# Other byte offsets for the matmul operands of a hybrid transformer block on one core

## The chip, the cores and the metric

The kernel runs on one core of a Trainium2 chip. The metric is the device time of one execution in microseconds, taken as the median of several runs. Each number of a trace comes from one profiled execution, whose span is the time from its first to its last instruction.

An SBUF address, in this document, is the byte at which a tile begins within its partition. All 128 partitions have the same layout, so one number says where a tile lies.

## The reference

One block of a hybrid network on 512 tokens with 1024 features, in fp32: a normalization, one wide input projection, two token mixers side by side (a gated delta rule with 8 heads and a retention with 4 heads), a gated sum of both, an output projection with a residual, and an MLP of width 4096 with a residual.

```python
xn = rmsnorm(x, n_mix_pre)
proj = xn @ w_in                       # 512 x 1024 by 1024 x 14352
qa, ka, va, za, beta_logit, a_dt, qb, kb, vb, gb, gate_a, gate_b = _split_cols(proj, IN_SIZES)
...
oa = chunk_gated_delta_rule(qa, ka, va, beta, g)
oa = rmsnorm(oa, norm_a) * jax.nn.silu(za)
ya = oa @ w_br_a
...
ob = chunk_retention(qb, kb, vb)
ob = rmsnorm(ob, norm_b) * jax.nn.silu(gb)
yb = ob @ w_br_b
mix = (jax.nn.sigmoid(gate_a) * ya + jax.nn.sigmoid(gate_b) * yb) @ w_out
x = x + rmsnorm(mix, n_mix_post)
hn = rmsnorm(x, n_mlp_pre)
ff = jnp.square(jax.nn.relu(hn @ w_up)) @ w_down
return x + rmsnorm(ff, n_mlp_post)
```

Most of the work is in the products with `w_in`, `w_br_a`, `w_br_b`, `w_out`, `w_up` and `w_down`.

## The kernel before

Every large product is made of three matmuls. A factor is split in two halves of type fp32r, a rounded one (`hi`) and the rest (`lo`), and `mm3` (lines 78 to 83) adds hi x hi (L81), hi x lo (L82) and lo x hi (L83) into one PSUM tile. The first operand of `nc.tensor.matmul` behind the output is the stationary one, which a LDWEIGHTS loads into the array ahead of the matmul (128 columns, 512 bytes of a partition); the second is the moving one, which streams through (mostly 512 columns, 2048 bytes of a partition). The trace names a matmul as output<-moving,stationary: `mm<-actT,whi` streams `actT` past weights from `whi`.

`weights` (lines 85 to 105) brings one block of weights: a DMA of 512 KB from SP's queue into a `raw` tile, ScalarE's rounding copy into `whi` (L100), VectorE's subtraction into `wlo` (L101). `whi` and `wlo` have three buffers each in the pool `ring`, so this work runs ahead of the matmuls by up to three blocks; a new block waits until the matmuls of the block three before it have ended. In a few places the halves go to other tiles, which the trace names `keep`.

Three functions use these blocks:

- `feature_major` (lines 107 to 125): the weights are stationary, the features move. The features are `actT` (two tiles of 8 x 512 columns, hi and lo; the normalized input in the first part of the kernel, later `mix` or the hidden layer), `og` (two tiles of 4 x 512 columns, a head's gated output) or `hn` (the normalized input of the MLP).
- `token_major` (lines 127 to 143): the features are stationary, the weights move. The trace shows `mm<-whi,actT` or `mm<-whi,ff`, where `ff` is the hidden layer. For two of the four groups of the MLP the hidden layer lies in a pair of `actT` tiles, for the other two in a pair of `og` tiles (first half) and a pair of tiles of the pool `pm` (second half).
- `row_tiles` (lines 824 to 850): as `token_major`, but with weights that stay on chip in `keep` tiles, for the output projection and the last group of the MLP.

Smaller products have no part in the change's own tiles: the transposes (L179), the plain fp32 products of the delta rule (L442 to L626), and the two products of retention, `dl<-qr,kr` and `dl<-vr,s`, which are `mm3` on tiles of the pool `pb`.

The order of instructions on each engine is made by a scheduler when the program is built, by the program's order and the priority that `weights` asks for. Tiles are laid out in SBUF pool after pool in the order in which pools are opened: constants (`cp`), `ring`, `act` (`actT` and `og`), `sm`, then a pool for each of the four parts, one after the other in the same space. A tile's address is therefore settled by the sizes of all the tiles before it, each rounded up to 32 bytes.

Of the kernel before, what the change touches and what calls it, by code (L numbers as in the profile page):

```python
# [10 lines left out]
F32 = mybir.dt.float32  # L11
F32R = mybir.dt.float32r
# [7 lines left out]
P = 128  # L20
# [7 lines left out]
OFF_GA, OFF_GBR = 12304, 13328  # L28
DFF = 4096


# [29 lines left out]
def hybrid_block_kernel(ctx: ExitStack, tc: tile.TileContext, a: dict, out: bass.AP):  # L61
# [5 lines left out]

    cp = ctx.enter_context(tc.tile_pool(name="cp", bufs=1))
    ring = ctx.enter_context(tc.tile_pool(name="ring", bufs=3))
    raw_pools = [ring]  # L70
# [5 lines left out]
    dr = ctx.enter_context(tc.tile_pool(name="dr", bufs=2, space=DRAM))  # L76

    def mm3(ps, lhs, rhs, first, last):
        lh, ll = lhs
        rh, rl = rhs  # L80
        nc.tensor.matmul(ps, lh, rh, start=first, stop=False)  # L81
        nc.tensor.matmul(ps, lh, rl, start=False, stop=False)  # L82
        nc.tensor.matmul(ps, ll, rh, start=False, stop=last)  # L83

    def weights(src, k0, nk, c0, ncols, keep=None):
        """nk blocks of 128 rows, ncols columns, in exact halves; split ahead of other work that is due."""
        n = nk * ncols
        i = next(loads)
        raw = raw_pools[i % len(raw_pools)].tile([P, 1024], F32, tag="raw", name="raw", bufs=2)
        nc.sync.dma_start(  # L90
            raw[:, :n].rearrange("p (k c) -> p k c", k=nk),
            src[k0 * P : (k0 + nk) * P, c0 : c0 + ncols].rearrange("(k p) c -> p k c", p=P),
        )
        if keep is None:
            hi = ring.tile([P, 1024], F32R, tag="whi", name="whi")
            lo = ring.tile([P, 1024], F32R, tag="wlo", name="wlo")
        else:
            hi, lo = keep
        with tc.high_priority(200 if i >= 6 else 0):
            nc.scalar.copy(hi[:, :n], raw[:, :n])  # L100
            nc.vector.tensor_tensor(lo[:, :n], raw[:, :n], hi[:, :n], ALU.subtract)  # L101
        return (
            hi[:, :n].rearrange("p (k c) -> p k c", k=nk),
            lo[:, :n].rearrange("p (k c) -> p k c", k=nk),
        )

    def feature_major(src, xs, c0, ncols, kts, krow0=0):
        """[feature, token] products of ncols columns: PSUM tiles of 128 features."""
        nf = ncols // P
        pss = [psm.tile([P, xs[0].shape[2]], F32, tag="mm", name="mm") for _ in range(nf)]  # L110
        step = 1024 // ncols
        for k0 in range(0, kts, step):
            wh, wl = weights(src, krow0 + k0, step, c0, ncols)
            for f in range(nf):
                fs = slice(f * P, (f + 1) * P)
                for kk in range(step):
                    kt = k0 + kk
                    mm3(
                        pss[f],
                        (wh[:, kk, fs], wl[:, kk, fs]),  # L120
                        (xs[0][:, kt, :], xs[1][:, kt, :]),
                        kt == 0,
                        kt == kts - 1,
                    )
        return pss

    def token_major(src, lhs, c0, kts, krow0=0):
        """[token, 512 columns] products: one PSUM tile for each 128 tokens."""
        pss = [psm.tile([P, T], F32, tag="mm", name="mm") for _ in range(4)]
        for k0 in range(0, kts, 2):  # L130
            wh, wl = weights(src, krow0 + k0, 2, c0, 512)
            for t in range(4):
                tt = slice(t * P, (t + 1) * P)
                for kk in range(2):
                    kt = k0 + kk
                    mm3(
                        pss[t],
                        [x[:, tt] for x in lhs(kt)],
                        (wh[:, kk, :], wl[:, kk, :]),
                        kt == 0,  # L140
                        kt == kts - 1,
                    )
        return pss
# [4 lines left out]
    def rsqrt(xv, n, name):  # L148
        """1/sqrt of a positive [P, n] tile."""
        yi = sm.tile([P, n], I32, tag=f"rs_i{n}", name="rs_i")  # L150
        y = sm.tile([P, n], F32, tag=f"rs_{name}", name="rs_y")
        t = sm.tile([P, n], F32, tag=f"rs_t{n}", name="rs_t")
        nc.vector.tensor_scalar(yi, xv.bitcast(I32), 1, None, ALU.logical_shift_right)
        nc.vector.tensor_scalar(y.bitcast(I32), yi, -1, 1597463007, ALU.mult, ALU.add)
        for _ in range(3):
            nc.vector.scalar_tensor_tensor(t, y, -0.5, y, ALU.mult, ALU.mult)
            nc.vector.tensor_tensor(t, t, xv, ALU.mult)
            nc.vector.scalar_tensor_tensor(y, t, 1.5, y, ALU.add, ALU.mult)
        return y
# [4 lines left out]

# [1 line left out]
    cmat = cp.tile([P, 3 * P], F32, name="cmat")  # L166
# [13 lines left out]

# [1 line left out]
    xs = [act.tile([P, 8, T], F32R, tag="actT", name="actT") for _ in range(2)]  # L182
    acc = cp.tile([P, 8, T], F32, name="acc")
# [7 lines left out]
    def root(v):  # L191
        """1/sqrt of a positive [P, n] tile."""
        n = v.shape[1]
# [9 lines left out]
    def rows_to_features(xn, t, dst):  # L203
        """Transposes the [128 tokens, 1024] tile into the halves dst."""
        tt = slice(t * P, (t + 1) * P)
# [9 lines left out]
    with tc.tile_pool(name="xp", bufs=2) as xp:  # L215
# [62 lines left out]

# [1 line left out]
        baT = xp.tile([16, T], F32, tag="baT", name="baT")  # L280
# [44 lines left out]
    def gate_rows(pss, o_t, zt):  # L325
        """o * rstd * silu(z) in place, token-major."""
        for t in range(4):
# [25 lines left out]

# [1 line left out]
    def conv_silu(ps, ch, dst, pool):  # L355
# [28 lines left out]
    def decays(h, pool):  # L384
        """exp(sum of g over (m, c]) for m <= c, else 1: [m, chunk, c]."""
        pd = psx.tile([P, T], F32, tag="dl", name="dl", bufs=3)
# [18 lines left out]
    with tc.tile_pool(name="pa", bufs=1) as pa:  # L405
# [46 lines left out]
        def base_inverse(g4, pool):  # L452
            """Unit lower triangular inverses of 64 diagonal 32-blocks, one to a partition."""
            scr_m, scr_r, scr_t = (dr.tile([4, 16, 1024], F32, tag=f"scr{i}", name="scr") for i in range(3))
# [33 lines left out]
        def double_blocks(pool, scr_r, m0):  # L488
            """From 32-blocks to the transposed 128-block inverses, for two heads."""
            rn = pool.tile([P, 8, 64], F32, tag="qf", name="rn", bufs=2)  # L490
# [42 lines left out]
        def values_queries(g2, pool):  # L533
# [33 lines left out]
            )  # L567
            # r_q * dk**-0.5
            rq = pool.tile([P, 8], F32, tag="rq", name="rq", bufs=2)
# [4 lines left out]
        def recurrence(g2, vq, pool):  # L574
# [61 lines left out]

            # rstd of the true output r_q * dk**-0.5 * o; a half of it for silu(z)
            v = pool.tile([P, 8], F32, tag="ov", name="ov")
# [40 lines left out]

# [1 line left out]
    with tc.tile_pool(name="pb", bufs=1) as pb_:  # L681
# [107 lines left out]
        for half in range(2):  # L789
# [5 lines left out]
            for f in range(4):  # L795
# [3 lines left out]
                nc.vector.tensor_tensor(acc[:, ft, :], acc[:, ft, :], m, ALU.add)  # L799
        mix = [act.tile([P, 8, T], F32R, tag="actT", name="actT") for _ in range(2)]  # L800
        for half, pss in branch_partial(w_br[1], prev, 12):
# [9 lines left out]

# [1 line left out]
    with tc.tile_pool(name="pm", bufs=1) as pm:  # L813
# [10 lines left out]
        def row_tiles(src, lhs, krow0, keeps, done):  # L824
            """[token, 1024] products, two tiles of 128 tokens and then one by one; the weights stay on chip."""
            kept = {}
# [27 lines left out]
        def norm_halves(parts):  # L854
            """rstd of rows that come in two halves; what else is done with a half may follow it."""
            ss = sm.tile([P, 2], F32, tag="nh_s", name="nh_s")
# [9 lines left out]
        def add_normed(t, parts, w):  # L866
            """x2[t] += rmsnorm(parts) * w."""
            fw = pm.tile([P, D], F32, tag="ym", name="fw", bufs=2)
# [58 lines left out]
        for grp in range(4):  # L927
            if grp % 2:
                whole = [act.tile([P, 8, T], F32R, tag="actT", name="actT") for _ in range(2)]
                ff = [[w[:, 4 * half : 4 * half + 4, :] for w in whole] for half in range(2)]  # L930
            else:
                ff = [
                    [act.tile([P, 4, T], F32R, tag="og", name="ff") for _ in range(2)],
                    [pm.tile([P, 4, T], F32R, tag=f"ff{i}", name="ff") for i in range(2)],
                ]
# [62 lines left out]
```

## Time and profile before

| What | Value |
|---|---|
| median of 3 runs | 1413.96 us (1412.99 to 1417.39) |
| span of the profiled execution | 1410.7 us |
| TensorE (PE) busy | 1394.6 us, 99% of the span |
| weight loads (PEld), beside the matmuls | 1139.7 us, 81% |
| VectorE (DVE) busy | 809.0 us, 57% |
| ScalarE (ACT) busy | 571.7 us, 41% |
| GpSimd (POOL) busy | 53.0 us, 4% |
| DMA | 129.74 MB, 92 GB/s on the mean |

The page gives no time of the profiled execution beyond its span. In its rows a group is named by line, engine, operation and tiles (written<-read), with the number of instructions, the time in which at least one of them ran, and the mean duration of one. Matmuls overlap: the next one starts before the one before it has ended, so the mean duration is longer than the distance between two starts. The order of time gives the start of each instruction in microseconds from the start of the span, to 10 ns; a distance between starts is worked out from the first and the last of many.

### The profile page before, as it was taken

Reading aid. Unit: us, or ns where it says so; the run is one execution under the profiler, and the core shown is the slowest. Engines: PE = TensorE matmul, PEld = TensorE weight load, DVE = VectorE, ACT = ScalarE, POOL = GpSimd, SP = SyncE. Lnnn points to the kernel's source line nnn. Section 1 sums busy time; section 2 is a strip of 40 time slices with the busy share of each in tenths; the row PEclk is TensorE's granted clock in tenths of the full one; section 3 lists DMA queues with packets and bytes.
Section 4 is the critical chain, followed back from the end, with each engine's and each line's share of the span. In section 5 each row is a group of like instructions: output and inputs, shape, how many; then the busy total and the mean of one; then the engine's idle time right before and its main releaser. Section 6 shows DMA issues by size and latency. Waiting matters only on the chain.

```text
span 1410.7 us, 17493 instructions
## 1 busy us (share of the span) xinstructions
PE 1394.6 (99%) x6766; PEld 1139.7 (81%) x6766; DVE 809.0 (57%) x1463; ACT 571.7 (41%) x1082; POOL 53.0 (4%) x100
## 2 busy tenths in 40 slices
PE   8999999999999999999999999999999999999997
PEld 6888787878888888888888888888888888888886
DVE  5599889944765564436445455445685333343445
ACT  6778564624534233233342323223464333132331
POOL 1111300200000000000000000000000000000000
PEclk9999999999999999999999999999999999999999
DMA  5232412221221342333223232232724232232321
GB/s 157 75 95 75 114 31 75 73 76 46 89 90 48 103 135 83 97 95 93 75 90 98 75 90 90 75 90 75 238 90 135 90 101 94 92 102 90 108 72 60
DMA packets 69942, 129.74 MB, mean 92 GB/s; under 512 B 4608, under 2 KB 18066, under 8 KB 69859
## 3 DMA queue, kind: packets, MB, share of 16 engines
q1 hardware_dynamic: 66128, 119.03, 26.8%
q0 software_dynamic: 3008, 8.34, 2.1%
q8 instruction: 53, 0.87, 0.3%
q10 hardware_dynamic: 722, 1.25, 0.2%
q14 instruction: 31, 0.25, 0.1%
HBM read 124.93 MB, written 3.67 MB: 91 GB/s over the span
## 4 chain that ended last, share of the span: by engine, by line
PE 92%; DVE 5%; ACT 1%; issue 1%; DMA 1%; SPq 0%; DVEq 0%; ACTq 0%
PE mm L81 27%; PE mm L82 27%; PE mm L83 27%; PE tr L179 2%; DVE c_y L367 1%; PE dl L83 1%; PE dl L82 1%; PE dl L81 1%; PE dl L598 1%; PE dl L626 1%; DVE wlo L101 1%; PE dl L590 1%; PE dl L606 1%; PE dl L619 1%; DVE tmp L473 1%
## 5 line engine op out<-in xcount | busy, mean ns | idle before, releaser
L101 DVE TENSOR_TENSOR wlo<-raw,whi 128x1024 fp32r<-128x1024 f32 x208 | 254.3, 1223 | 387.8 <-ACT whi L100 386.6
L100 ACT CAST whi<-raw 128x1024 fp32r<-128x1024 f32 x208 | 218.3, 1050 | 514.0 <-PE mm L82 282.1
L82 PE MATMUL mm<-actT,whi 128*128 128x512 f32 (+1 forms) x528 | 207.7, 393 | 1.2 <-DVE actT L213 1.2
L81 PE MATMUL mm<-actT,whi 128*128 128x512 f32 (+1 forms) x528 | 206.8, 393 | 1.0 <-ACT actT L212 1.0
L83 PE MATMUL mm<-actT,wlo 128*128 128x512 f32 (+1 forms) x528 | 207.3, 393 | 0.0
L81 PE MATMUL mm<-whi,actT 128*128 128x512 f32 x472 | 185.9, 394 | 0.1
L82 PE MATMUL mm<-wlo,actT 128*128 128x512 f32 x472 | 185.4, 393 | 0.0
L83 PE MATMUL mm<-whi,actT 128*128 128x512 f32 x472 | 185.2, 393 | 0.0
L81 PEld LDWEIGHTS mm<-actT,whi 128*128 128x128 f32 x528 | 99.8, 189 | 21.4 <-ACT actT L212 1.3
L82 PEld LDWEIGHTS mm<-actT,whi 128*128 128x128 f32 x528 | 100.1, 190 | 20.4 <-DVE actT L213 1.4
L83 PEld LDWEIGHTS mm<-actT,wlo 128*128 128x128 f32 x528 | 100.0, 189 | 19.0
L81 PE MATMUL mm<-hn,whi 128*128 128x512 f32 (+1 forms) x288 | 106.3, 370 | 0.6 <-DVE r L921 0.5
L82 PE MATMUL mm<-hn,whi 128*128 128x512 f32 (+1 forms) x288 | 106.2, 369 | 0.0
L83 PE MATMUL mm<-hn,wlo 128*128 128x512 f32 (+1 forms) x288 | 106.0, 369 | 0.0
L81 PEld LDWEIGHTS mm<-whi,actT 128*128 128x128 f32 x472 | 88.6, 188 | 19.0 <-ACT c_y L365 0.5
L83 PEld LDWEIGHTS mm<-whi,actT 128*128 128x128 f32 x472 | 88.6, 188 | 18.2
L82 PEld LDWEIGHTS mm<-wlo,actT 128*128 128x128 f32 x472 | 88.6, 188 | 17.9
L81 PE MATMUL mm<-og,whi 128*128 128x512 f32 x256 | 100.3, 392 | 0.0
L82 PE MATMUL mm<-og,whi 128*128 128x512 f32 x256 | 99.6, 389 | 0.0
L83 PE MATMUL mm<-og,wlo 128*128 128x512 f32 x256 | 98.5, 390 | 0.0
L367 DVE SCALAR_TENSOR_TENSOR c_y<-c_raw,convw,c_y 128x512 f32<-128x512 f32 x96 | 70.5, 752 | 3.4 <-ACT c_y L365 2.8
L81 PEld LDWEIGHTS mm<-hn,whi 128*128 128x128 f32 x288 | 54.0, 187 | 11.4 <-issue 0.7
(286 smaller groups left out, 2077.0 us busy)
## 6 DMA issues: line engine op xcount, KB each, us to landing
raw<-in_w_in_dram SPq DMA_DIRECT2D x113, 512.0 KB, 3.6
raw<-in_w_up_dram SPq DMA_DIRECT2D x36, 512.0 KB, 3.6
raw<-in_w_down_dram SPq DMA_DIRECT2D x32, 512.0 KB, 3.6
raw<-in_w_br_a_dram SPq DMA_DIRECT2D x16, 512.0 KB, 3.6
raw<-in_w_br_b_dram SPq DMA_DIRECT2D x16, 512.0 KB, 3.6
raw<-in_w_out_dram SPq DMA_DIRECT2D x8, 512.0 KB, 3.7
x<-in_x_dram SPq DMA_DIRECT2D x4, 512.0 KB, 6.4
acc<-in_x_dram POOLq DMA_DIRECT2D x4, 512.0 KB, 3.8
```

What stands on the lines that cost most here:

```text
L81: nc.tensor.matmul(ps, lh, rh, start=first, stop=False)
L82: nc.tensor.matmul(ps, lh, rl, start=False, stop=False)
L83: nc.tensor.matmul(ps, ll, rh, start=False, stop=last)
L100: nc.scalar.copy(hi[:, :n], raw[:, :n])
L101: nc.vector.tensor_tensor(lo[:, :n], raw[:, :n], hi[:, :n], ALU.subtract)
L179: nc.tensor.transpose(ps, src, ident)
L367: nc.vector.scalar_tensor_tensor(y, raw[:, j : j + T], tap(j), y, ALU.mult, ALU.add)
L473: nc.vector.tensor_tensor(t3, mb3[:, j, j + 1 : 32].unsqueeze(2).to_broadcast([64, nr, ni]), rb3[:, j, 0:ni].unsqueeze(1).to_broadcast([64 ...
L590: nc.tensor.matmul(ks[:, hh, :], kf[:, h0 + hh, cs], state[:, hh, :], start=True, stop=True)
L598: nc.tensor.matmul(px[:, hh, :], rt[:, nn[hh], :], vx[:, hh, :], start=True, stop=True)
L606: nc.tensor.matmul(pc[:, hh, :], kd[:, nn[hh], :], vn[:, hh, :], start=True, stop=True)
L619: nc.tensor.matmul(qs[:, hh, :], qf[:, hh, cs], prev[:, hh, :], start=True, stop=True)
```

## The change

It adds 56 fp32 columns (224 bytes) of an unused tile at the start of the pool `cp`, and 8 fp32 columns (32 bytes) behind each `whi`, `wlo` and `actT` tile. The columns that are added are neither written nor read. All the rest of the program, its instructions, shapes, buffers and order, is the same; what differs is the address of nearly every tile.

```diff
+STAGGER = 8
...
     cp = ctx.enter_context(tc.tile_pool(name="cp", bufs=1))
+    cp.tile([P, 56], F32, name="shift")
     ring = ctx.enter_context(tc.tile_pool(name="ring", bufs=3))
...
+    def features_tile(name):
+
+        w = act.tile([P, 8 * T + STAGGER], F32R, tag="actT", name=name)
+        return w[:, : 8 * T].rearrange("p (k t) -> p k t", k=8)
...
-            hi = ring.tile([P, 1024], F32R, tag="whi", name="whi")
-            lo = ring.tile([P, 1024], F32R, tag="wlo", name="wlo")
+            hi = ring.tile([P, 1024 + STAGGER], F32R, tag="whi", name="whi")
+            lo = ring.tile([P, 1024 + STAGGER], F32R, tag="wlo", name="wlo")
...
-    xs = [act.tile([P, 8, T], F32R, tag="actT", name="actT") for _ in range(2)]
+    xs = [features_tile("actT") for _ in range(2)]
...
-        mix = [act.tile([P, 8, T], F32R, tag="actT", name="actT") for _ in range(2)]
+        mix = [features_tile("actT") for _ in range(2)]
...
-                whole = [act.tile([P, 8, T], F32R, tag="actT", name="actT") for _ in range(2)]
+                whole = [features_tile("actT") for _ in range(2)]
```

The addresses in the built programs, in bytes, whole and modulo 512. Every operand of a matmul begins at a multiple of 512 bytes from the start of its tile (a column block of 128 fp32, or a row of 512), so the modulo of the tile is that of each operand in it.

| Tile | before | mod 512 | after | mod 512 |
|---|---|---|---|---|
| `raw`, 2 buffers | 36896, 40992 | 32, 32 | 37120, 41216 | 256, 256 |
| `whi`, 3 buffers | 45088, 49184, 53280 | 32, 32, 32 | 45312, 49440, 53568 | 256, 288, 320 |
| `wlo`, 3 buffers | 57376, 61472, 65568 | 32, 32, 32 | 57696, 61824, 65952 | 352, 384, 416 |
| `actT`, hi and lo | 69664, 86048 | 32, 32 | 70080, 86496 | 448, 480 |
| `og`, hi and lo | 102432, 110624 | 32, 32 | 102912, 111104 | 0, 0 |
| `hn`, hi and lo | 128736, 145120 | 224, 224 | 129216, 145600 | 192, 192 |
| `ff` of pool pm, hi and lo | 161504, 169696 | 224, 224 | 161984, 170176 | 192, 192 |
| `qr`, `kr`, `vr`, `s` (retention) | | 224 | | 192 |
| `later` (stationary of L391) | 18624 | 192 | 18848 | 416 |
| `kf`, `kd`, `rt` (delta rule) | 120544, 136928, 153312 | 224 | 121024, 137408, 153792 | 192 |
| end of the SBUF in use | 228384 | | 228864 | |

`keep` tiles lie in the space of `og`, `ff`, `hn` and `facc` and have their offsets.

## The prediction

> **What bounds the kernel now.** I read the page's busy times first, then the granted clock, then the chain that ended last, then the groups kept apart by shape.
>
> ```profile
> span 1410.7 us, 17493 instructions
> PE 1394.6 (99%) x6766; PEld 1139.7 (81%) x6766; DVE 809.0 (57%) x1463; ACT 571.7 (41%) x1082; POOL 53.0 (4%) x100
> PEclk9999999999999999999999999999999999999999
> PE 92%; DVE 5%; ACT 1%; issue 1%; DMA 1%; SPq 0%; DVEq 0%; ACTq 0%
> PE mm L81 27%; PE mm L82 27%; PE mm L83 27%; PE tr L179 2%; DVE c_y L367 1%; PE dl L83 1%; PE dl L82 1%; PE dl L81 1%; PE dl L598 1%; PE dl L626 1%; DVE wlo L101 1%; PE dl L590 1%; PE dl L606 1%; PE dl L619 1%; DVE tmp L473 1%
> ```
>
> TensorE is busy 99% of the span at full clock, and the three matmuls of `mm3` (L81 to L83) make 81% of the chain. There is almost no idle time to win or lose, so the time is the number of these matmuls times the distance from the start of one to the start of the next. A matmul's mean duration (some 390 ns) says little, because they overlap. The distance has to be taken from start times:
>
> ```profile
> 587.03 0.39 PE L81 MATMUL mm<-actT,whi 128*128 128x512 f32 x1
> 630.33 0.40 PE L83 MATMUL mm<-actT,wlo 128*128 128x512 f32 x1
> ```
>
> These are the first and the last of 192 matmuls in one unbroken stretch: 43.30 us / 191 = 226.7 ns. Here both operands stand at byte 32 of 512 (the table in the section on the change). The stretches with other offsets lie in the MLP:
>
> ```profile
> 1103.84 0.39 PE L81 MATMUL mm<-whi,ff 128*128 128x512 f32 x1
> 1114.83 0.39 PE L81 MATMUL mm<-whi,ff 128*128 128x512 f32 x1
> 1125.70 0.39 PE L81 MATMUL mm<-whi,ff 128*128 128x512 f32 x1
> 1136.69 0.39 PE L81 MATMUL mm<-hn,whi 128*128 128x512 f32 x1
> 1181.49 0.39 PE L81 MATMUL mm<-whi,actT 128*128 128x512 f32 x1
> ```
>
> From 1103.84 to 1114.83 lie 48 matmuls, the moving operand at byte 32 and the stationary one at 224 (`ff` tiles of pool pm): 10.99 / 48 = 229.0 ns. From 1114.83 to 1125.70 lie 48 more of the same line and tile names, but now `ff` is a pair of `og` tiles at byte 32: 10.87 / 48 = 226.5 ns. From 1125.70 it is 224 again: 10.99 / 48 = 229.0 ns. From 1136.69 to 1181.49 lie 192 with moving `hn` at 224 and stationary `whi` at 32: 44.80 / 192 = 233.3 ns. Same shape, same clock, no idle time: what differs is the byte offset. The mean duration of one, in windows of the pure stretches, marks the same difference; the third row is from the view of one tile (least, median, most):
>
> ```profile
> L81 PE MATMUL mm<-actT,whi 128*128 128x512 f32 x64 | 24.9, 389 | 0.0
> L81 PE MATMUL mm<-hn,whi 128*128 128x512 f32 x64 | 25.2, 394 | 0.0
> L81 PE MATMUL dl<-vr,s x40: 389/389/391, 536.4 to 886.3; 128*128 128x512 f32 x40
> ```
>
> `vr` and `s` both stand at 224 and last as long as two operands at 32. So it is not the place of one operand that goes with the time but the difference. I call moving minus stationary, modulo 512, the phase: 0 costs 226.7 ns, 192 costs 233.3, 320 costs 229.0.
>
> Why the operands can meet at all:
>
> ```profile
> 590.21 0.39 PE L83 MATMUL mm<-actT,wlo 128*128 128x512 f32 x1
> 590.21 0.19 PEld L81 LDWEIGHTS mm<-actT,whi 128*128 128x128 f32 x1
> 590.43 0.39 PE L81 MATMUL mm<-actT,whi 128*128 128x512 f32 x1
> 590.43 0.19 PEld L82 LDWEIGHTS mm<-actT,whi 128*128 128x128 f32 x1
> ```
>
> The weight load of the next matmul starts with the present matmul, so both read SBUF side by side. The plain fp32 matmuls show how short the distance can be; their phases are 160 and 0:
>
> ```profile
> 181.01 1.03 PE L619 MATMUL dl<-st,qf 128*128 128x256 f32 x4
> 181.88 1.03 PE L626 MATMUL dl<-vn,at 128*128 128x256 f32 x4
> L619 PE MATMUL dl<-st,qf x48: 379/379/379, 181.0 to 446.1; 128*128 128x256 f32 x48
> ```
>
> Four in 1.03 us, one lasting 379 ns, give (1.03 - 0.38) / 3 = 217 ns. They take as long for 256 columns as the others for 512, so they fetch the moving operand at half the rate, and phase doesn't show. Against that floor the 512-wide matmuls pay some 10 ns at phase 0 and 16 at phase 192.
>
> The Trainium skill ("TensorE: Matmul & The Clock Gate", "Wait — 56ns, not 53.3ns?") states 215.7 ns for a warm 512-column matmul; every stretch above is 11 to 18 ns over it.
>
> **The change part by part.** No instruction is added, removed or moved: each engine issues the same list, SP's and POOL's queues too, and no wait changes. The tile `shift` is never written. Three things remain.
>
> First, the transfers and the splitting of weights, whose tiles now start at other bytes.
>
> ```profile
> L101 DVE TENSOR_TENSOR wlo<-raw,whi 128x1024 fp32r<-128x1024 f32 x208 | 254.3, 1223 | 387.8 <-ACT whi L100 386.6
> L100 ACT CAST whi<-raw 128x1024 fp32r<-128x1024 f32 x208 | 218.3, 1050 | 514.0 <-PE mm L82 282.1
> raw<-in_w_in_dram SPq DMA_DIRECT2D x113, 512.0 KB, 3.6
> ```
>
> I cost it at nothing. ScalarE's copy waits 282 us in all for L82 to free a buffer, so TensorE sets the pace of the ring. The cover is that wait. A 10% longer pair would add 0.23 us to each block of 24 matmuls (5.4 us), where the chain already holds only 1% of L101; were that 1% to grow by a tenth, it would cost 1.4 us, and as much less if the pair got faster.
>
> Second, the larger tiles: the SBUF in use grows by 480 bytes in a partition and still fits, so no pool loses a buffer.
>
> Third, the phases of the matmuls, the whole of the case. The groups and what they have now:
>
> ```profile
> L81 PE MATMUL mm<-actT,whi 128*128 128x512 f32 x512 | 201.7, 395 | 0.0
> L81 PE MATMUL mm<-whi,actT 128*128 128x512 f32 x472 | 185.9, 394 | 0.1
> L81 PE MATMUL mm<-og,whi 128*128 128x512 f32 x256 | 100.3, 392 | 0.0
> L81 PE MATMUL mm<-hn,whi 128*128 128x512 f32 x224 | 88.2, 395 | 0.0
> L81 PE MATMUL mm<-whi,ff 128*128 128x512 f32 x128 | 50.0, 391 | 0.0
> L81 PE MATMUL mm<-keep,actT 128*128 128x512 f32 x104 | 40.9, 394 | 0.0
> ```
>
> Each count stands three times (L81, L82, L83): 5,088 matmuls. At phase 0 are the first three groups (3,720), half of `ff` (192) and the `keep` blocks in `og` tiles (96): 4,008. At phase 192 are `hn` (672) and the other `keep` (some 213): 885. At 320 is the other half of `ff`, 192. Their average is (4,008 x 226.7 + 885 x 233.3 + 192 x 229.0) / 5,085 = 227.9 ns. Afterwards the phase changes with the buffer, from about -192 to +192 in steps of 32; almost nothing keeps phase 0, and some 300 stand at exactly 256. The products of retention (`vr` with `s`, `qr` with `kr`) keep theirs, since both their tiles move together.
>
> No trace shows a 512-wide matmul in a steady stretch at 64, 96, 128, 160 or 256, so their price is bounded. The upper end is the dearest steady row, 233.3: 4,008 x 6.6 + 192 x 4.3 = +27.3 us. The lower end is the fp32 floor of 217, were the streams never to meet: 5,085 x (217 - 227.9) = -55 us. A gain isn't excluded, because 256-wide matmuls go the other way:
>
> ```profile
> 25.00 0.28 PE L81 MATMUL mm<-actT,whi 128*128 128x256 f32 x1
> 26.68 0.28 PE L83 MATMUL mm<-actT,wlo 128*128 128x256 f32 x1
> 1048.91 0.28 PE L81 MATMUL mm<-hn,whi 128*128 128x256 f32 x1
> 1049.70 0.28 PE L82 MATMUL mm<-hn,whi 128*128 128x256 f32 x1
> ```
>
> Phase 0: 1.68 / 14 = 120 ns. Phase 192: 0.79 / 7 = 113 ns, 7 less. But there a weight load (0.19 us) outlasts the matmul's turn, which no 512-wide one does. So I weigh the three rows of unequal phase 9 : 9 : 2, in ns against phase 0: 0.45 x 6.6 + 0.45 x 2.3 - 0.1 x 7 = +3.3. The price taken is 230.0 ns. The sum: 4,008 x 3.3 = +13.2; 885 x (230.0 - 233.3) = -2.9; 192 x 1.0 = +0.2; the 192 `hn` matmuls of 256 columns move by half of their 7 ns, +0.7. Together +11 us.
>
> The profiled execution spans 1410.7 us and so comes to 1421.8; its span lies 3.3 us under the median of 1413.96, and the same 11 us on that give 1425.
>
> **The rivals.**
>
> *The new phases keep the streams apart (faster).* The place is every 512-wide `mm3`; the price is that of the 256-wide rows, 226.7 - 7 = 219.7 ns on average: 5,085 x (219.7 - 227.9) = -42 us, 1372 us. For it: 120 against 113 ns, and the 10 ns above the floor that phase 0 pays. Against it: both steady 512-wide rows of unequal phase are dearer than phase 0. It decides as soon as the average price falls below 227.9; a partial form, `hn` and `keep` down to 226.7 and the rest unchanged, gives -885 x 6.6 = -5.8 us, 1408 us.
>
> *Unequal is unequal (slower, fully).* All pay 233.3: 1441 us. For it: `hn` and `keep` pay it for hundreds of matmuls on end. Against it: `ff` at 320 pays a third of that.
>
> *Offsets don't matter or cancel (same).* 1414 us. The distances would then belong to stages. Against it: within one stage, 1103.84 to 1136.69, the distance goes 229.0, 226.5, 229.0 as only the `ff` tile changes. Cancelling needs an average between 227.1 and 228.7 ns (0.3% of the time, 4.2 us, over 5,085), which single prices from 217 to 233 allow. The Trainium skill (the same page, "Step-by-step: what each phase is for") says that moving operand and weight load have independent read ports and that loading steals no bandwidth from the running matmul; by that rule the result would be this rival's. Those three distances disagree with it by 2.5 ns, and `hn` by 6.6.
>
> **How the numbers follow.** Between the middle price and the full one lie most outcomes: 0.58 that it is slower by over 0.3% (0.3% is about what a measurement of this kernel can tell from no change). Offsets without effect or cancelling: 0.14. Faster: 0.28, of which 0.13 for the full form and 0.15 for partial ones. The range reaches from 1396, where the partial forms end, to 1442, just above the full price; that leaves out the full gain and about 0.06 above. The likeliest case alone has 1418 to 1441.
>
> **What would show it.** PE's share stays 99% and its instruction count 6766; L100 and L101 keep 1050 and 1223 ns. The stretch of 192 `actT,whi` matmuls near 587 us takes about 44.2 us instead of 43.5, and the distance jumps from one block of 24 matmuls to the next with the buffer. The `hn` stretches shorten a little. Wrong would be: a stretch of `actT,whi` under 226 ns a matmul (the first rival), no steps between blocks (the third), or idle time of PE in front of `whi` (then the first part was mispriced).

## The result and the profile after

The changed kernel takes 1427.34 us in the median of 3 runs (1427.18 to 1429.46), against 1413.96 us: a ratio of 1.0093 with a 95% interval of 1.0074 to 1.0113. It is 13.4 us slower; 1425 us, 11 us slower, was forecast.

The page of the changed kernel, from its first, fourth and fifth part. The seven lines that the diff adds ahead of them move L81 to L83 to L88 to L90, and L100 and L101 to L107 and L108.

```profile
span 1425.6 us, 17493 instructions
PE 1408.2 (99%) x6766; PEld 1142.1 (80%) x6766; DVE 809.9 (57%) x1463; ACT 571.9 (40%) x1082; POOL 55.2 (4%) x100
PE 92%; DVE 3%; DMA 2%; ACT 1%; POOL 1%; issue 1%; SPq 0%; DVEq 0%; ACTq 0%
L108 DVE TENSOR_TENSOR wlo<-raw,whi 128x1024 fp32r<-128x1024 f32 x208 | 254.5, 1224 | 396.5 <-ACT whi L107 395.6
L107 ACT CAST whi<-raw 128x1024 fp32r<-128x1024 f32 x208 | 217.9, 1049 | 526.1 <-PE mm L89 288.4
```

The span grew by 14.9 us and PE's busy time by 13.6. Instruction counts, PE's share of the span and of the chain, and the durations of the two instructions that split the weights are those of before. So the same matmuls, still without idle time, follow each other at longer distances. The order of time on PE, same view as in the prediction (start in us, duration in us):

```profile
593.12 0.40 PE L88 MATMUL mm<-actT,whi 128*128 128x512 f32 x1
598.71 0.39 PE L88 MATMUL mm<-actT,whi 128*128 128x512 f32 x1
604.23 0.39 PE L88 MATMUL mm<-actT,whi 128*128 128x512 f32 x1
609.75 0.39 PE L88 MATMUL mm<-actT,whi 128*128 128x512 f32 x1
615.34 0.39 PE L88 MATMUL mm<-actT,whi 128*128 128x512 f32 x1
637.26 0.39 PE L90 MATMUL mm<-actT,wlo 128*128 128x512 f32 x1
...
1117.27 0.39 PE L88 MATMUL mm<-whi,ff 128*128 128x512 f32 x1
1128.34 0.39 PE L88 MATMUL mm<-whi,ff 128*128 128x512 f32 x1
1139.43 0.40 PE L88 MATMUL mm<-whi,ff 128*128 128x512 f32 x1
1150.54 0.39 PE L88 MATMUL mm<-hn,whi 128*128 128x512 f32 x1
1195.11 0.40 PE L88 MATMUL mm<-whi,actT 128*128 128x512 f32 x1
```

Each row of the first five starts a block of 24 matmuls with a `whi` and a `wlo` from the next of the three buffers. The blocks take 5.59, 5.52, 5.52 and again 5.59 us: 233, 230, 230 and 233 ns a matmul, in step with the ring. The whole stretch of 192 is (637.26 - 593.12) / 191 = 231.1 ns a matmul, where it was 226.7. The `hn` stretch is 44.57 / 192 = 232.1 ns (233.3 before); the blocks of `ff` take 11.07 and 11.09 us (10.99 and 10.87 before).

The differences between the starts of all 6,766 matmuls, summed by group, tell where the 14.9 us come from (changed kernel minus before; a group holds the distances between 512-wide matmuls that are under 0.28 us in both kernels, and all others stand in the last row):

| group (moving / stationary) | us |
|---|---|
| `actT` / weights | +4.7 |
| weights / `actT` | +5.5 |
| `og` / weights | +3.6 |
| weights / `ff` | +1.2 |
| `keep` / `actT` | +0.2 |
| `hn` / weights | -0.8 |
| everything else (256-wide, start, transposes, small products, breaks) | +0.5 |

### The profile page after: what moved, and what is told of

The parts are those of the page before. It is cut to its first block, busy times and chain, and to the rows that moved or that the text cites. A ratio compares the mean times of both kernels' runs of the same rounds, so it can differ in the third digit from the quotient of the medians.

```text
span 1425.6 us, 17493 instructions
## 1 busy us (share of the span) xinstructions
PE 1408.2 (99%) x6766; PEld 1142.1 (80%) x6766; DVE 809.9 (57%) x1463; ACT 571.9 (40%) x1082; POOL 55.2 (4%) x100
## 4 chain that ended last, share of the span: by engine, by line
PE 92%; DVE 3%; DMA 2%; ACT 1%; POOL 1%; issue 1%; SPq 0%; DVEq 0%; ACTq 0%
PE mm L88 27%; PE mm L89 27%; PE mm L90 27%; PE tr L186 2%; PE dl L90 1%; PE dl L89 1%; PE dl L88 1%; PE dl L605 1%; PE dl L633 1%; PE dl L613 1%; PE dl L597 1%; PE dl L626 1%; DMA raw<-in_w_out_dram 1%; POOL at L572 1%; DMA x<-in_x_dram 1%; DVE wlo L108 1%
## 5 line engine op out<-in xcount | busy, mean ns | idle before, releaser
L108 DVE TENSOR_TENSOR wlo<-raw,whi 128x1024 fp32r<-128x1024 f32 x208 | 254.5, 1224 | 396.5 <-ACT whi L107 395.6
L107 ACT CAST whi<-raw 128x1024 fp32r<-128x1024 f32 x208 | 217.9, 1049 | 526.1 <-PE mm L89 288.4
L88 PE MATMUL mm<-actT,whi 128*128 128x512 f32 (+1 forms) x528 | 209.1, 397 | 0.6 <-ACT actT L219 0.6
L90 PE MATMUL mm<-actT,wlo 128*128 128x512 f32 (+1 forms) x528 | 208.9, 396 | 0.0
L88 PE MATMUL mm<-whi,actT 128*128 128x512 f32 x472 | 188.0, 398 | 0.1
L90 PE MATMUL mm<-whi,actT 128*128 128x512 f32 x472 | 186.4, 395 | 0.0
L88 PEld LDWEIGHTS mm<-actT,whi 128*128 128x128 f32 x528 | 100.1, 190 | 22.3 <-ACT actT L219 0.9
L90 PEld LDWEIGHTS mm<-actT,wlo 128*128 128x128 f32 x528 | 100.4, 190 | 20.9
L88 PE MATMUL mm<-hn,whi 128*128 128x512 f32 (+1 forms) x288 | 106.7, 371 | 0.6 <-DVE r L928 0.5
L90 PE MATMUL mm<-hn,wlo 128*128 128x512 f32 (+1 forms) x288 | 105.9, 369 | 0.0
L90 PEld LDWEIGHTS mm<-whi,actT 128*128 128x128 f32 x472 | 88.9, 188 | 20.3
L88 PEld LDWEIGHTS mm<-whi,actT 128*128 128x128 f32 x472 | 88.5, 188 | 20.6 <-ACT c_y L372 0.5
L88 PE MATMUL mm<-og,whi 128*128 128x512 f32 x256 | 101.7, 397 | 0.0
L90 PE MATMUL mm<-og,wlo 128*128 128x512 f32 x256 | 99.4, 393 | 0.0
L88 PEld LDWEIGHTS mm<-hn,whi 128*128 128x128 f32 x288 | 54.1, 188 | 11.0 <-issue 0.7
```

## The experiments

The theory: the distance between two 512-wide fp32r matmuls depends on the difference between the byte offsets of moving and stationary operand (the phase), not on where either lies. The rivals: the place of an operand counts; unequal offsets would be the cheapest ones; a difference costs the same whatever its size; what counts is that neighbours in the order of matmuls have other offsets. Ratios are to the kernel before, on the same chip. Distances are taken from two rows as above, or, where no row stands beside them, from the starts of all matmuls of the stretch or group that is named.

**e1: every tile moved by the same 224 bytes.**

```diff
     cp = ctx.enter_context(tc.tile_pool(name="cp", bufs=1))
+    cp.tile([P, 56], F32, name="shift")
```

> The kernel before with the 224 unused bytes alone, so that every tile moves by 224 bytes and no difference between two operands changes. Phase theory (the price of a matmul goes with moving minus stationary start, modulo 512): nothing changes, 1414 us, 226.7 ns a matmul in the actT stretch near 587 us, 233.3 ns with hn. Place theory (the price goes with the byte at which one operand starts, and the tiles at 32 or 224 were cheap or dear by their place): all tiles have a new place, and both distances change by several ns; 1 ns on each of the 5,085 matmuls is 5 us.

1413.07 us, ratio 0.9994 (0.9985 to 1.0003). The same stretches in the order of time of e1:

```profile
586.75 0.39 PE L82 MATMUL mm<-actT,whi 128*128 128x512 f32 x1
630.05 0.40 PE L84 MATMUL mm<-actT,wlo 128*128 128x512 f32 x1
...
1137.85 0.39 PE L82 MATMUL mm<-hn,whi 128*128 128x512 f32 x1
1182.64 0.39 PE L82 MATMUL mm<-whi,actT 128*128 128x512 f32 x1
```

43.30 / 191 = 226.7 ns and 44.79 / 192 = 233.3 ns, as before. All addresses are others and nothing happens: the place of an operand doesn't count.

**e2: the 32 bytes behind each tile, without the shift.** The changed kernel less one line:

```diff
-    cp.tile([P, 56], F32, name="shift")
```

> The changed kernel without the 224 bytes: each whi, wlo and actT tile has 32 bytes behind it, and the differences between tiles of the ring, actT, og and hn are those of the changed kernel. Phase theory: 1427 us as the changed kernel. Place theory: another time than the changed kernel's, since whi now starts at 32, 64 and 96 and not at 256, 288 and 320; between 1414 and 1427 or beyond.

1427.96 us, ratio 1.0101 (1.0088 to 1.0115), with the changed kernel's distances (231.1 ns in the stretch of `actT`, 232.1 in that of `hn`). The 32 bytes are the whole of the case.

**e3: all operands at the same offset.** The kernel before with 320 bytes at the start of the pool `pm`, which bring `hn`, `ff` and the `keep` tiles of that pool from 224 to 32, where the weights and the other features stand:

```diff
     with tc.tile_pool(name="pm", bufs=1) as pm:
+        pm.tile([P, 80], F32, name="padm")
```

> The kernel before with 320 unused bytes at the start of pool pm alone, so that hn, ff and the keep tiles of pm start at byte 32 of 512 like whi, wlo, actT and og: phase 0 everywhere. Phase theory: 885 matmuls fall from 233.3 to 226.7 ns (-5.8 us), 192 of ff from 229.0 to 226.7 (-0.4 us), and the 192 of 256 columns rise from 113 to 120 ns (+1.3 us): -4.9 us, 1409 us. If the distance belonged to the stage and not to the offsets: 1414 us, and 233 ns with hn as before.

1408.10 us, ratio 0.9961 (0.9949 to 0.9974): 0.4% faster than the kernel before, 1.3% faster than the changed one. In the order of time of e3:

```profile
1116.09 0.39 PE L81 MATMUL mm<-whi,ff 128*128 128x512 f32 x1
1126.97 0.39 PE L81 MATMUL mm<-whi,ff 128*128 128x512 f32 x1
1137.85 0.39 PE L81 MATMUL mm<-hn,whi 128*128 128x512 f32 x1
1181.37 0.39 PE L81 MATMUL mm<-whi,actT 128*128 128x512 f32 x1
1224.89 0.39 PE L81 MATMUL mm<-hn,whi 128*128 128x512 f32 x1
```

10.88 / 48 = 226.7 ns for both blocks of `ff`, and 43.52 / 192 = 226.7 ns for `hn` and for `actT`. The two prices of before, 233.3 and 229.0, are gone with the differences.

The kernels e4 to e7, e9 and e10 are e3 with one more unused tile ahead of the features in the pool `act`, `N` fp32 columns wide. All features then lie 4 x N bytes behind the weights. Feature-major matmuls (features move) have that phase, token-major ones (weights move) its negative.

```diff
     act = ctx.enter_context(tc.tile_pool(name="act", bufs=2))
+    act.tile([P, N], F32, name="pada", bufs=1)
```

**e4: 192 bytes (N = 48).**

> The kernel with phase 0 everywhere, and then 192 unused bytes in front of actT and og, so that all features start 192 bytes behind all weights, modulo 512: one constant phase of +192 where weights are stationary and of 320 (-192) where features are. Phase theory, by the prices seen before the change: 233.3 ns in the actT stretch near 587 us and with og and hn, 229.0 ns in each token-major stretch; against the kernel before, 2,304 x 6.6 = +15.2 us, 1,608 x 2.3 = +3.7 us, 213 keep matmuls back to phase 0 = -1.4 us: 1431 us. Rival (not the phase but its changing from matmul to matmul is what costs): a constant phase costs no more than phase 0, 1409 us.

1426.43 us, ratio 1.0088 (1.0074 to 1.0102). In the order of time of e4:

```profile
591.56 0.40 PE L82 MATMUL mm<-actT,whi 128*128 128x512 f32 x1
636.13 0.41 PE L84 MATMUL mm<-actT,wlo 128*128 128x512 f32 x1
1116.38 0.40 PE L82 MATMUL mm<-whi,ff 128*128 128x512 f32 x1
1127.58 0.40 PE L82 MATMUL mm<-whi,ff 128*128 128x512 f32 x1
...
1194.78 0.40 PE L82 MATMUL mm<-whi,actT 128*128 128x512 f32 x1
1238.74 0.39 PE L82 MATMUL mm<-hn,whi 128*128 128x512 f32 x1
```

Moving `actT` at +192 pays what `hn` paid at that phase: 44.57 / 191 = 233.4 ns. The other direction, at -192, pays 43.96 / 192 = 229.0 ns, as `ff` did at 320. So these prices go with the phase and not with the tile, and the rival that only a changing phase costs (1409 us) has fallen. The 1431 us expected were 4.6 too many: the sum took the whole of the `actT` group to stand at 226.7 ns, but over all of them the kernel before has 228.0, and some 1.8 us were gained outside these groups, 1.0 of them in the first 30 us. One row pair doesn't fit: the weights moving past `ff`, also at -192, pay 11.20 / 48 = 233.3 ns, all of them, where the kernel before had 229.0 at the same difference. e6 has another such case.

**e5: 256 bytes (N = 64).**

> As the kernel with the features 192 bytes apart, but 256: constant phase 256, the same in both directions. If the price repeats every 256 bytes: 226.7 ns as at phase 0, 1408 us. If it repeats only every 512 bytes: another price; the changed kernel has 232.6 ns on the mean in the og matmuls at 256, which with 3,700 matmuls (+5 ns) gives 1427 us.

1408.22 us, ratio 0.9957 (0.9943 to 0.9971). In the order of time of e5:

```profile
588.08 0.39 PE L82 MATMUL mm<-actT,whi 128*128 128x512 f32 x1
631.37 0.40 PE L84 MATMUL mm<-actT,wlo 128*128 128x512 f32 x1
...
1182.06 0.39 PE L82 MATMUL mm<-whi,actT 128*128 128x512 f32 x1
1225.58 0.39 PE L82 MATMUL mm<-hn,whi 128*128 128x512 f32 x1
```

226.6 ns feature-major and 226.7 token-major: operands 256 bytes apart are as good as equal ones. The phase is to be taken modulo 256, not 512.

**e6: 64 bytes (N = 16).**

> Features 64 bytes behind the weights: phase +64 where weights are stationary, 448 (-64) where features are. If the price repeats every 256 bytes, the directions change places against the kernel with 192: feature-major stretches about 229 ns (as 320), token-major stretches 233.3 (as 192); 2,304 x 2 + 1,608 x 6 = +14 us over the kernel with phase 0 everywhere (1408), 1422 us. If a distance of 64 is as good as none (only multiples of 64 bytes mattered): 1408 us.

1422.15 us, ratio 1.0059 (1.0044 to 1.0074). In the order of time of e6:

```profile
590.59 0.39 PE L82 MATMUL mm<-actT,whi 128*128 128x512 f32 x1
634.31 0.40 PE L84 MATMUL mm<-actT,wlo 128*128 128x512 f32 x1
...
1190.56 0.39 PE L82 MATMUL mm<-whi,actT 128*128 128x512 f32 x1
1235.36 0.39 PE L82 MATMUL mm<-hn,whi 128*128 128x512 f32 x1
```

43.72 / 191 = 228.9 ns feature-major, 44.80 / 192 = 233.3 token-major. Against e4 the two directions have changed places, as they must if -192 is the same as +64 modulo 256.

The price at 64 has a second value, though. These are the first and the last rows of two stretches of 96 matmuls in e6, in which the same `og` tiles move past the weights at the same +64:

```profile
405.03 0.40 PE L82 MATMUL mm<-og,whi 128*128 128x512 f32 x1
427.20 0.40 PE L84 MATMUL mm<-og,wlo 128*128 128x512 f32 x1
...
984.85 0.39 PE L82 MATMUL mm<-og,whi 128*128 128x512 f32 x1
1006.59 0.39 PE L84 MATMUL mm<-og,wlo 128*128 128x512 f32 x1
```

The first pays 22.17 / 95 = 233.4 ns, the second 21.74 / 95 = 228.8. At 64 a stretch thus takes one of two prices and keeps it to its end, as the `ff` stretch of e4 does; the offsets don't decide which, and what does stays open.

**e7: 128 bytes (N = 32).**

> Features 128 bytes behind the weights: +128 and 384 (-128). If the price repeats every 256 bytes, both directions have one price; if every 128 bytes, that is phase 0's: 226.7 ns and 1408 us. From the changed kernel's mixture (231.6 ns on the mean at 128 and 384): 3,900 x 4.9 = +19 us over 1408, 1427 us. A rival that wants the streams apart: the greatest distance within 256 bytes is the cheapest, under 226.7 ns and under 1408 us.

1430.11 us, ratio 1.0112 (1.0097 to 1.0127). Modulo 256 both directions stand at 128 here. In the order of time of e7:

```profile
594.33 0.39 PE L82 MATMUL mm<-actT,whi 128*128 128x512 f32 x1
638.72 0.40 PE L84 MATMUL mm<-actT,wlo 128*128 128x512 f32 x1
...
1198.20 0.40 PE L82 MATMUL mm<-whi,actT 128*128 128x512 f32 x1
1243.00 0.40 PE L82 MATMUL mm<-hn,whi 128*128 128x512 f32 x1
```

232.4 and 233.3 ns, and 3 us more than the 1427 expected. The two values don't belong to the two directions: moving `actT` has 232.4 ns here and 233.3 in a later stretch (749.08 to 764.71 us, 68 matmuls), past weights from the same ring. So 128, too, has two prices for the same tiles and offsets. The phase farthest from equal is among the dear ones; that it would be the cheapest has fallen.

**e8: only `wlo` apart.** e3 with 320 bytes ahead of the `wlo` buffers, and 192 ahead of the features, so that these keep `whi`'s offset modulo 512:

```diff
             hi = ring.tile([P, 1024], F32R, tag="whi", name="whi")
+            if i == 0:
+                ring.tile([P, 80], F32, name="padw", bufs=1)
             lo = ring.tile([P, 1024], F32R, tag="wlo", name="wlo")
...
+    act.tile([P, 48], F32, name="pada", bufs=1)
```

> The kernel with phase 0 everywhere, and wlo alone 320 bytes on. In feature-major blocks only the third matmul of a product (lo x hi) uses wlo, and its weights load while the second runs. If the running matmul meets the weights that are being loaded for the next one, the second is long (phase 192, up to 233.3 ns) and the third short (226.7). If it meets its own weights, the third is long and the second short. One of three long: on the mean up to 229 ns, some 2,976 x 2.2 = +6.5 us in these blocks, and in token-major blocks wlo is the moving operand of the second (phase 320, 229 to 233 ns, one in three): +1 to +3 us; 1415 to 1418 us.

1425.63 us, ratio 1.0079 (1.0064 to 1.0094), where 1415 to 1418 were expected. In the order of time of e8:

```profile
592.40 0.39 PE L82 MATMUL mm<-actT,whi 128*128 128x512 f32 x1
636.54 0.40 PE L84 MATMUL mm<-actT,wlo 128*128 128x512 f32 x1
```

44.14 / 191 = 231.1 ns. One matmul of three has an unequal phase, and the mean rises by 4.4 ns instead of a third of 6.6. By line, in this stretch, the distances from the first, second and third matmul of a product to the next start are 228.3, 229.1 and 236.0 ns on the mean (226.0, 227.0 and 227.0 in the same stretch of e3): all three grow, those at phase 0 too. So prices of steady phases don't add up when the phase changes from one matmul to the next. e8 was also to tell whether a matmul meets the load of its own weights or of the next one's. The long one is the third, as if it met its own; but it is longer than a steady phase 192 (233.3), and the other two grew by some 2 ns each, so neither form holds as it was put, and this isn't shown.

**e11: the control for e8.** The same two tiles with 64 columns each; `wlo` lies 256 bytes off instead of 320.

```diff
-                ring.tile([P, 80], F32, name="padw", bufs=1)
+                ring.tile([P, 64], F32, name="padw", bufs=1)
...
-    act.tile([P, 48], F32, name="pada", bufs=1)
+    act.tile([P, 64], F32, name="pada", bufs=1)
```

> The control for e8: the wlo tiles lie 256 bytes off (288 of 512) where e8 had them 320 off, everything else as there. If in e8 the difference of offsets modulo 256 did it, all operands stand equal here and the kernel comes to e3's and e5's 1408 us, all three matmuls of a product at 226.7 to 228 ns. If it was that whi and wlo don't lie at the same offset modulo 512, so that consecutive matmuls change their offsets, it stays near e8's 1425.6.

1408.19 us, ratio 0.9961 (0.9947 to 0.9976). In the order of time of e11:

```profile
586.91 0.39 PE L82 MATMUL mm<-actT,whi 128*128 128x512 f32 x1
630.21 0.40 PE L84 MATMUL mm<-actT,wlo 128*128 128x512 f32 x1
```

43.30 / 191 = 226.7 ns. Halves of weights at different addresses cost nothing as long as the difference is a multiple of 256.

**e9 and e10: 32 and 96 bytes (N = 8 and 24).** All that the changed kernel adds is steps of 32 bytes, and no steady price for an odd multiple of 32 had been seen.

> e3 with the feature tiles 32 bytes behind the weights: feature-major matmuls at +32, token-major ones at -32 (224 of 256). Steady prices so far: 226.7 ns at 0 and 256, 229.4 at +64, 232.5 at 128, 233.3 at 192 (-64). If the price goes smoothly with the difference modulo 256, feature-major comes to some 228 ns, token-major to some 230, and the kernel to about 1415 us (e4 and e6 together give a weight of 2,290 feature-major and 1,190 token-major matmuls: 2.29 x 1.3 + 1.19 x 3.3 = 6.9 us on e3's 1408.1). If any difference that isn't a multiple of 64 bytes is dear (a rival with steps), both directions stand at 232 to 233 ns and the kernel at 1427 to 1431.

> e3 with the feature tiles 96 bytes behind the weights: feature-major at +96, token-major at -96 (160 of 256). Smooth prices: feature-major between 229.4 (+64) and 232.5 (128), some 231; token-major between 232.5 (128) and 233.3 (192), some 233; the kernel about 1425 us (2.29 x 4.3 + 1.19 x 6.3 = 17.3 us on 1408.1). With steps at multiples of 64 bytes: feature-major as at 64 or as at 128, 1421 or 1430.

e9: 1433.26 us, ratio 1.0137 (1.0120 to 1.0154). e10: 1434.79 us, ratio 1.0146 (1.0131 to 1.0161). In the order of time, first e9, then e10:

```profile
594.32 0.39 PE L82 MATMUL mm<-actT,whi 128*128 128x512 f32 x1
638.89 0.39 PE L84 MATMUL mm<-actT,wlo 128*128 128x512 f32 x1
...
1198.74 0.40 PE L82 MATMUL mm<-whi,actT 128*128 128x512 f32 x1
1243.55 0.39 PE L82 MATMUL mm<-hn,whi 128*128 128x512 f32 x1
```

```profile
596.77 0.39 PE L82 MATMUL mm<-actT,whi 128*128 128x512 f32 x1
641.33 0.40 PE L84 MATMUL mm<-actT,wlo 128*128 128x512 f32 x1
...
1202.44 0.40 PE L82 MATMUL mm<-whi,actT 128*128 128x512 f32 x1
1247.42 0.40 PE L82 MATMUL mm<-hn,whi 128*128 128x512 f32 x1
```

233.4 and 233.4 ns in e9, 233.3 and 234.3 in e10. The smooth course (1415 us for e9, 1425 for e10) was wrong, and 32 bytes cost as much as 192. For e9 the rival with steps comes closest (232 to 233 ns, 1427 to 1431 us); its upper end lies 2 us under the measured time. For e10 it is further off (1421 or 1430): 96 has the dearer of the two prices of 128, and 160 more than either. Odd multiples of 32 have the full price or a little over.

The steady prices, by moving minus stationary offset modulo 256:

| phase | ns | seen in |
|---|---|---|
| 0 | 226.7 | e3, e5, e11 |
| 32 | 233.4 | e9 |
| 64 | 229.0; in some stretches 233.3 | before (`ff`), e4, e6; 233.3 for `ff` in e4 and one stretch of `og` in e6 |
| 96 | 233.3 | e10 |
| 128 | 232.4 or 233.3 | e7 |
| 160 | 234.3 | e10 |
| 192 | 233.3 | before (`hn`), e4, e6 |
| 224 | 233.4 | e9 |

## Why the prediction was right

*The first part, splitting and transfers at nothing: right.* L107 and L108 have 1049 and 1224 ns, their means of before within 1 ns, and PE has 99% of the span. e1, which moves every `raw`, `whi` and `wlo` tile and keeps the phases, changes nothing either.

*The third part, the phases: right in mechanism, a little short in size.* Without the table's last row, the average price over the 5,085 matmuls is 227.9 + 14.4 / 5.085 = 230.7 ns where 230.0 was taken. Against the span the sum is 3.7 us short (11.2 of 14.9), against the medians 2.2 (11.2 of 13.4), as the changed kernel's span lies 1.7 us under its median and not 3.3.

*The terms that were mis-sized.* The three groups that stood wholly at phase 0 (`actT`, weights / `actT`, `og`) were to lose 3,720 x 3.3 = 12.3 us and lost 13.8. The one that returns time, 885 x (230.0 - 233.3) = -2.9 us, was worse: the `hn` stretch fell to 232.1 ns only, which over its 672 matmuls is -0.8 us of the -2.2 that were its share, and the `keep` group, whose gain at 213 matmuls was to outweigh the loss at 96 by 0.4 us, grew by 0.2. `ff` lost 1.2 us where 0.8 was taken, the 256-wide `hn` matmuls 0.2 where 0.7 was. The 0.3 us that are left lie outside these groups, where nothing was taken.

*The weighing 9 : 9 : 2 gave nearly the right price for a wrong reason.* It took two kinds of unequal phase for equally frequent, a cheap one (229.0) and a dear one (233.3), with a small share for a gain. The runs show the cheap one at a single phase of eight, 64, and there not in every stretch, and no gain at any. So the size came out nearly right by luck. With the steady prices of the table, the matmuls of the changed kernel counted by their phase would average 232.4 ns; over the same matmuls its trace has 231.6. Phases that change from matmul to matmul cost less there than the steady ones would, and in e8 they cost more (231.2 measured, 228.3 by the table). How prices combine is not settled.

*What was to be seen.* The stretch near 587 us was to take 44.2 us, which is 192 distances; it takes 44.14 from its first start to its last, which is 191, and so 44.4 by the same count. The steps from block to block are there, 5.59, 5.52, 5.52, 5.59 us. e11, whose `whi` and `wlo` lie 256 bytes apart modulo 512, has 226.7 ns, so that different places alone cost nothing. The `hn` stretch shortened, by 0.23 us.

*The rivals.* "Keep the streams apart" has fallen: no steady 512-wide phase is cheaper than 0, in eight phases tried. Its evidence, the 256-wide matmuls, was true of the rows shown and carried no further: there e3 goes from 113 to 120 ns as `hn` comes to phase 0, while the 512-wide ones gain 6.6 ns; and later in the same `hn` stretch of the kernel before, at the same phase, they have 117.8. "Unequal is unequal" (1441 us) is the better rule for a phase held steady, 64 excepted: e9, with its features 32 bytes off, comes to 1433. For the changed kernel, where phases alternate, it is too dear. "Offsets don't matter or cancel" has fallen for the 512-wide ones. The rule named beside it from the Trainium skill ("TensorE: Matmul & The Clock Gate", "Step-by-step: what each phase is for"), that a weight load takes no bandwidth from the running matmul, would leave the distance as it is whatever the offsets. For these fp32r matmuls the distance does change: e3 and e9 differ in nothing but 32 bytes of offset, and stand at 226.7 and 233.4 ns. That it is the load and the stream that meet in SBUF was argued from their overlap in the trace; the runs show the dependence on the two offsets, not the place where it arises.

## What to carry to other kernels

Where TensorE is busy all the time with matmuls like these, look at the addresses of moving and stationary operands, and bring them to the same offset modulo 256 bytes: a tile of 320 unused bytes ahead of one pool made this kernel 0.4% faster than before (e3), and 32 more ahead of the features made that 1.8% slower (e9, 1433.26 against 1408.10). A pool that follows others inherits the sum of all their sizes, so one small tile anywhere can set or spoil it. Take the price from distances between starts in long unbroken stretches (0.01 us over 191 matmuls is 0.05 ns), not from durations of matmuls that overlap.

## What was not expected of the hardware

The period is 256 bytes, and within it the course is neither smooth nor symmetric: 226.7 ns at 0, 229.0 at 64 in most stretches, 232.4 to 234.3 at the six others. At 64 and 128 the same tiles at the same offsets have one of two prices from stretch to stretch. Prices are not properties of a single matmul: in e8, with one phase of three unequal, the two at phase 0 grew as well. The 256-wide matmuls go another way, worked out from the starts of the same `hn` stretch: 120 ns at equal offsets (e3) and also at 96 (e10), 117 at 32 (e9), and at 192 (before) 113.5 in its first part and 117.8 in its last.
